# One decoder layer on one NeuronCore: constant pool shortened by 128 bytes, RWKV output splits and first down products in another order

## The chip, the core and the metric

The kernel runs on one NeuronCore of a Trainium2 chip. Its time is the device time of one launch in microseconds (us), read on the chip. The engines are named as the profile names them: PE (TensorE, matrix products), PEld (the loads of PE's stationary operand, which run beside products), DVE (VectorE), ACT (ScalarE), POOL (GpSimd) and SP (SyncE, here the issuer of nearly all DMA transfers). Each engine runs its own instruction list in order, and lists meet at semaphores.

## The reference, cut to what matters

```python
h = rms_norm(x, norm1_w) * (1 + sc1) + sh1          # x: (512, 1024), sc/sh/gt from c @ w_ada
proj = h @ w_in                                      # attention, RWKV and gate columns
y_att = attention_mixer(att_in) @ w_att_out
y_rwkv = rwkv7_mixer(rwkv_in, ...) @ w_rwkv_out
x = x + gt1 * ((sig(g_att) * y_att + sig(g_rwkv) * y_rwkv) @ w_o)
h = rms_norm(x, norm2_w) * (1 + sc2) + sh2
u = conv_b + sum(conv_w[j] * shifted(h @ w_up)[j])   # w_up: (1024, 5632), causal width 3
x = x + gt2 * ((silu(u_gate) * u_val) @ w_down)      # w_down: (2816, 1024)
out = rms_norm(x, norm_f_w)
```

All of it is float32. The kernel keeps that precision by splitting each operand of the large products into a rounded high part and the remainder, and by adding three products: high by high, high by low, low by high.

## The kernel before, in words

**Products.** A large product takes 128 rows of contraction at a time; the moving operand has 512 columns, the stationary one 128. `gemm_ks` (lines 432 to 439) and `tok_gemm` issue the three products per 128 rows, all through line 415, so the profile groups them by tile names: `u<-h2hi,whi` is a product into u with h2hi moving and whi stationary. In the up projection the activations h2 move and the weights stand; in the down projection and the `w_o` product the weights move and the activations (f, mhi and mlo) stand.

**Weight splits.** `load_w` brings 512 KB of raw weights into the ring `raw` (two buffers, pool `wp`). `split_w` (lines 456 to 462) has ACT copy the high part (line 460) and DVE subtract it for the low part (line 461). The results go into `whi` and `wlo`, two buffers each, which come free when PE has used them.

**Memory.** Pools stand at the left-hand end of SBUF, one behind the other, or at the right-hand end. The first left-hand pool, `cp`, holds constants; `vec_rest` (lines 531 to 555) makes nine scaled copies of parameter columns in it. All left-hand pools behind it (weights, `hp` with the first norm's output, `fp` with f) start where `cp` ends. The right-hand pools hold h2, the RWKV output y (`yhi`, `ylo`), and the extra weight buffers `we` of the last down products.

**RWKV output.** `rwkv_out` runs with an order written out by hand. For the eight 128-column blocks m of the mixed output, PE multiplies y by `w_rwkv_out` (`pr`), DVE applies the gate (`added`, line 2441), adds the attention branch (line 2445), ACT makes mhi (line 2446), and DVE makes mlo (line 2449). Between them stand the splits of the `w_rwkv_out` blocks 5 to 7, of the eight row blocks of `w_o` (`split_wo`), and of the first `w_up` blocks. `mix_out` then forms the four token blocks n of `(...) @ w_o`, the residual, the second norm and, through transposes on PE (line 418), h2: DVE scales into `hf` (line 626), ACT copies h2hi (line 631), POOL subtracts h2lo (line 632). The residual tile x of n = 0 lies where the gate tiles of m = 6 and 7 were, so its load on SP (line 2532) waits for the last use of these, the mlo of m = 7.

**FFN.** `ffn_first` does the first up block for 384 tokens, then the last 128 tokens when their h2 is there. `ffn_up` runs over f = 0 to 21; for each f two halves z (gate and value), each 24 products, then the convolution on ACT and DVE (`u`, lines 2599 and 2601), SiLU, and the split of f into fhi and flo. In the iteration f = 20 stands the split of the first `w_down` row block, from a raw buffer of its own (`rawd`) in the pool `up`; a scheduler places each instruction in its engine's list, and this one stands early, as the lists below show. `ffn_down` accumulates over 22 row blocks k for four token blocks n, two halves each, in eight PSUM banks, two of which hold the last `u` until DVE has read it. The first eight (k, n) pairs stand in a written order.

Of the kernel before, what the change touches and what calls it, by code (L numbers as in the profile page):

```python
# [19 lines left out]
P = 128  # L20
S = 512
D = 1024
# [373 lines left out]
class Layer:  # L396
# [134 lines left out]
    def vec_rest(self, deps):  # L531
# [3 lines left out]

        def scaled(name, m, a):
            s = self.col[name]
            o = cp.tile([P, s.shape[1]], F32, name=self.n(name))
            todo.append((o, s, m, a))
            return o  # L540

        self.omu = scaled("mu", -1.0, 1.0)
        self.omu2 = scaled("mu2", -1.0, 1.0)
        self.w0h = scaled("w0", 0.5, 0.0)
        self.a0h = scaled("a0", 0.5, 0.0)
        self.kkn = scaled("k_k", -1.0, 0.0)
        self.kkh = scaled("k_k", 0.5, 0.0)
        self.kah = scaled("k_a", 0.5, 0.0)
        self.kao = scaled("k_a", -0.5, 1.0)
        self.bgh = scaled("b_gate", 0.5, 0.0)  # L550

# [1871 lines left out]
    def rwkv_out(self, mpool, wpool, psp):  # L2423
# [15 lines left out]
        def added(m):  # L2439
            t, pr = self.tr_[m], ahead[m]["pm"]  # L2440
            nc.vector.scalar_tensor_tensor(t, t, 1.0, pr, op0=ALU.add, op1=ALU.mult)

        def mixed(m):
            t = self.tr_[m]
            nc.vector.tensor_tensor(t, t, self.p[m], op=ALU.add)
            nc.scalar.activation(self.mhi[:, m, :], t, AF.Copy, scale=0.5)
# [5 lines left out]
        with self.tc.manual_schedule(engines={T.PE, T.DVE, T.Activation, T.Pool, T.SP}):  # L2452
# [27 lines left out]
            for m in range(3, KD):  # L2480
                if m > 4:
                    ahead[m]["pm"] = psp("pr")
                prod(ahead[m]["w"], ahead[m]["pm"], range(KD))
                if m == 5:
                    ahead.append(dict(w=self.split_w(raw)))
                self.split_wo()
                if m + 1 < KD:
                    self.load_wo(wpool, m + 1)
                if m == KD - 1:
                    self.split_wo()  # L2490
                added(m)
                mixed(m)
                mixed_lo(m)
# [96 lines left out]
    def ffn_up(self, fp, up, psx):  # L2590
# [13 lines left out]
        for f in range(NFF):  # L2604
# [5 lines left out]
            if f == NFF - 2:  # L2610
                raw = self.load_w(self.w_down[0][:P, :], 1, D, up, tag="rawd", bufs=1)
                self.fp, self.wd0 = fp, [x[:, 0, :] for x in self.split_w(raw, pool=fp, tag="wd")]
            us = [conv(z, f, pus[z]) for z in range(2)]
# [4 lines left out]
    def ffn_down(self, xp, op, psx):  # L2618
# [9 lines left out]
        w = {0: self.wd0, 1: self.row_w(self.w_down[0], 1)}  # L2628
        for k, n in ((0, 0), (0, 1), (0, 2), (1, 0), (0, 3), (1, 1), (1, 2), (1, 3)):
            self.tok_gemm(pt[n], n, fk, w, [k], NFF)  # L2630
# [182 lines left out]
```

## Time and profile before

| what | value |
|---|---|
| median of three runs | 1175.56 us (1174.59 to 1177.84) |
| the profiled execution's own time | 1174.78 us |
| its span, first to last instruction | 1173.1 us |
| PE busy | 1156.1 us, 99% |
| DVE, ACT, POOL busy | 739.2, 536.1, 134.9 us |
| up projection, f = 1 to 21 | 810.12 to 1044.36 us of the span |
| down projection | 1044.36 us to the end |
| mean granted TensorE clock | 0.997 |

How to read it: a row of the timeline has start, duration, engine, source line, operation and tiles, and in brackets the idle time before it with what ended it. Durations of products are modelled and overlap the next one; the time that a product costs in a dense run is the distance between starts. A span on PE that is 99% busy can hence still hold products that start later after each other than others do.

### The profile page before, as it was taken

The numbers are of one execution on the slowest core, as the hardware profiler recorded it, in microseconds if no ns is written. First come the engines' busy times: TensorE is split into PE (matmuls) and PEld (weight loads), VectorE is DVE, ScalarE is ACT, GpSimd is POOL, SyncE is SP. The second block draws the span as 40 slices with busy tenths as digits, with TensorE's granted clock in tenths as the row PEclk, the third lists the DMA queues.
The fourth block names the chain that finished last, engine by engine and source line by source line (L and its number), as shares of the span: only waits on it lengthen the run. The fifth ranks groups of instructions, "written<-read, shape, count | busy, mean of one in ns | idle before, by whom it ended". The sixth has DMA issues, their size and how long they took to land.

```text
span 1173.1 us, 18932 instructions
## 1 busy us (share of the span) xinstructions
PE 1156.1 (99%) x7432; PEld 927.9 (79%) x7432; DVE 739.2 (63%) x1268; ACT 536.1 (46%) x1013; POOL 134.9 (12%) x272
## 2 busy tenths in 40 slices
PE   9999999999999999999999999999999999999997
PEld 7888887887777777778777668788888888878886
DVE  6788756315799968458996456755656556542236
ACT  5566526216564554455365553445444444432123
POOL 6000000001200033221003330032000000000001
PEclk9999999999999999999999999999999999999999
DMA  9656663311342423223223536611333333332331
GB/s 363 216 179 222 218 212 109 92 37 44 99 113 64 117 86 108 67 84 103 74 74 115 157 114 228 203 55 54 91 90 94 104 90 90 97 101 90 94 122 73
DMA packets 161820, 139.01 MB, mean 118 GB/s; under 512 B 8513, under 2 KB 141761, under 8 KB 161730
## 3 DMA queue, kind: packets, MB, share of 16 engines
q1 hardware_dynamic: 161586, 137.47, 37.7%
q8 instruction: 58, 0.95, 0.3%
q14 instruction: 32, 0.26, 0.1%
q10 hardware_dynamic: 144, 0.33, 0.1%
HBM read 127.47 MB, written 10.30 MB: 117 GB/s over the span
## 4 chain that ended last, share of the span: by engine, by line
PE 46%; DVE 3%; issue 1%; ACT 1%; DMA 0%; POOL 0%; POOLq 0%; DVEq 0%; ACTq 0%
PE u L415 21%; PE o L415 12%; PE pr L415 3%; PE pg L415 3%; PE pa L415 2%; PE xy L415 1%; PE xo L415 1%; PE pe L415 1%; DMA raw<-in_w_o_dram 0%; DVE tt L1839 0%; DVE tt L1837 0%; PE t L415 0%; DVE wlo L461 0%; DVE hf L626 0%; DVE wlo L1462 0%
## 5 line engine op out<-in xcount | busy, mean ns | idle before, releaser
L461 DVE TENSOR_TENSOR wlo<-raw,whi 128x1024 fp32r<-128x1024 f32 x64 | 78.4, 1224 | 145.6 <-ACT whi L460 145.6
L415 PE MATMUL u<-h2hi,whi 128*128 128x512 f32 (+2 forms) x364 | 141.7, 389 | 0.8 <-ACT h2hi L631 0.8
L415 PE MATMUL u<-h2lo,whi 128*128 128x512 f32 (+2 forms) x364 | 141.7, 389 | 0.2 <-POOL h2lo L632 0.2
L415 PE MATMUL u<-h2hi,wlo 128*128 128x512 f32 (+2 forms) x364 | 141.5, 389 | 0.0
L1462 DVE TENSOR_TENSOR wlo<-raw,whi 128x1024 fp32r<-128x1024 f32 (+1 forms) x73 | 84.5, 1158 | 45.7 <-ACT whi L1459 45.2
L460 ACT CAST whi<-raw 128x1024 fp32r<-128x1024 f32 x64 | 67.1, 1049 | 99.2 <-PE o L415 54.8
L1459 ACT CAST whi<-raw 128x1024 fp32r<-128x1024 f32 (+1 forms) x73 | 72.4, 993 | 69.8 <-PE qk L415 11.2
L415 PEld LDWEIGHTS u<-h2hi,whi 128*128 128x128 f32 x364 | 68.6, 188 | 15.9 <-ACT h2hi L631 1.1
L415 PEld LDWEIGHTS u<-h2lo,whi 128*128 128x128 f32 x364 | 68.6, 188 | 15.3 <-POOL h2lo L632 0.3
L415 PEld LDWEIGHTS u<-h2hi,wlo 128*128 128x128 f32 x364 | 68.6, 188 | 15.0
L571 DVE CUSTOM_DVE_ANT_0 araw<-araw,cb,cols 128x1024 f32<-128x1024 f32 x48 | 61.4, 1287 | 15.4 <-DMA araw<-in_w_ada_dram 15.3
L2601 DVE SCALAR_TENSOR_TENSOR u<-u,cols,u 128x511 f32<-128x511 f32 x88 | 65.6, 746 | 1.5
L415 PE MATMUL qk<-hhi,whi 128*128 128x512 f32 x160 | 64.1, 406 | 0.2
L415 PE MATMUL qk<-hhi,wlo 128*128 128x512 f32 x160 | 62.8, 395 | 0.0
L415 PE MATMUL qk<-hlo,whi 128*128 128x512 f32 x160 | 62.6, 396 | 0.0
L415 PE MATMUL o<-whi,fhi 128*128 128x512 f32 x136 | 52.9, 389 | 0.0
L415 PE MATMUL o<-wlo,fhi 128*128 128x512 f32 x136 | 52.9, 389 | 0.0
L415 PE MATMUL o<-whi,flo 128*128 128x512 f32 x136 | 52.9, 389 | 0.0
L415 PE MATMUL pg<-hhi,whi 128*128 128x512 f32 x128 | 51.7, 411 | 1.0 <-DVE k L1472 0.8
L415 PE MATMUL pg<-hlo,whi 128*128 128x512 f32 x128 | 51.5, 408 | 0.0
L415 PE MATMUL pg<-hhi,wlo 128*128 128x512 f32 x128 | 50.7, 405 | 0.0
L1112 ACT ACTIVATE pr<-sm,stat 128x256 f32<-128x256 f32 (+1 forms) x64 | 31.4, 491 | 36.2 <-PE pt L418 19.8
(465 smaller groups left out, 2729.1 us busy)
## 6 DMA issues: line engine op xcount, KB each, us to landing
raw<-in_w_in_dram SPq DMA_DIRECT2D x62, 512.0 KB, 3.9
araw<-in_w_ada_dram SPq DMA_DIRECT2D x48, 512.0 KB, 5.8
raw<-in_w_up_dram SPq DMA_DIRECT2D x44, 512.0 KB, 3.6
raw<-in_w_down_dram SPq DMA_DIRECT2D x22, 512.0 KB, 3.4
wvraw<-in_w_in_dram SPq DMA_DIRECT2D x20, 256.0 KB, 4.1
raw<-in_w_rwkv_out_dram SPq DMA_DIRECT2D x8, 512.0 KB, 4.5
raw<-in_w_o_dram SPq DMA_DIRECT2D x8, 512.0 KB, 4.1
gate_d<-gs SPq DMA_DIRECT2D x15, 256.0 KB, 2.1
```

The source lines that it names most:

```text
L415: return self.nc.tensor.matmul(out, lhsT, rhs, start=start, stop=stop)
L460: self.nc.scalar.copy(hl[0], raw)
L461: (lo_eng or self.nc.vector).tensor_tensor(hl[1], raw, hl[0], op=ALU.subtract)
L571: self.nc.vector.tensor_tensor_reduce(raw, raw, self.cb, 1.0, self.col["b_ada"][:, m : m + 1], op0=ALU.mult, op1=ALU.add, accum_out=col)
L1112: nc.scalar.activation(d["pr"][h][:, :wd], d["sm", h][:, :wd], AF.Exp, bias=stt[gi][:, n, 0, hd(h) : hd(h) + 1], scale=-1.0, accum_out=stt ...
L1459: nc.scalar.copy(d["w"][0], d["raw"])
L1462: nc.vector.tensor_tensor(d["w"][1], d["raw"], d["w"][0], op=ALU.subtract)
L2601: nc.vector.scalar_tensor_tensor(u[:, d:], pu[:, : S - d], ch(c), u[:, d:], op0=ALU.mult, op1=ALU.add)
```

## The change

Three edits.

1. Three of the nine scaled columns (w0, a0, b_gate) are written in place over their source columns instead of into new tiles. `cp` becomes 32 + 32 + 64 = 128 bytes per partition shorter, and every left-hand pool behind it moves down by 128 bytes. Right-hand pools stay. In the built programs the tiles of the large products then start as follows (address modulo 256 bytes, moving / stationary):

| product | before | after |
|---|---|---|
| up, f = 1 to 21 (h2 / w) | 128 / 0 | 128 / 128 |
| up, f = 0, z = 0 (h2 / w) | 128 / 0 | 128 / 128 |
| up, f = 0, z = 1 (h2 / w of a right-hand pool) | 128 / 128 | 128 / 128 |
| down, k = 0 to 18 (w / f) | 0 / 0 | 128 / 128 |
| down, k = 19 to 21 (we / f) | 128 / 0 | 128 / 128 |
| RWKV output (y / w) | 128 / 0, for most | 128 / 128, for most |
| `w_o` product (wo / m) | 0 / 0 | 128 / 128 |
| projections by `w_in` (h / w) | 0 / 0 | 128 / 128 |

Counting, over the whole program, the 512-column moving operand of one product against the stationary operand of the next product: 2241 pairs agree modulo 256 before and 3561 after; 1471 are 128 apart before and 151 after. Of the 1471, 1009 are in the up projection, 165 in the RWKV output, 79 in the attention output (`pa`), 63 in the down projection.

2. In `rwkv_out` the products of m = 5 are written ahead with those of m = 4, and with them the split of the last `w_rwkv_out` block (m = 7); the last `w_o` split is written behind the gate steps of m = 7. PE's order of the `pr` products is the same as before. DVE's list around the gate steps of m = 4, first before, then after (`wlo<-raw,whi` in the first rows is the split for m = 7, wolo those of `w_o`, gate and mlo the gate steps):

```order
L2449 SCALAR_TENSOR_TENSOR mlo<-gate_7576,mhi 128x512
L2309 TENSOR_TENSOR wolo_7720<-raw_7659,wohi_7719 128x1024
L2441 SCALAR_TENSOR_TENSOR gate_7577<-gate_7577,pr_7598 128x512
L2445 TENSOR_TENSOR gate_7577<-gate_7577,gate_6991 128x512
L2449 SCALAR_TENSOR_TENSOR mlo<-gate_7577,mhi 128x512
L461 TENSOR_TENSOR wlo_7755<-raw_7657,whi_7754 128x1024
```

```order
L2449 SCALAR_TENSOR_TENSOR mlo<-gate_7573,mhi 128x512
L461 TENSOR_TENSOR wlo_7742<-raw_7654,whi_7741 128x1024
L2309 TENSOR_TENSOR wolo_7746<-raw_7656,wohi_7745 128x1024
L2441 SCALAR_TENSOR_TENSOR gate_7574<-gate_7574,pr_7595 128x512
L2445 TENSOR_TENSOR gate_7574<-gate_7574,gate_6988 128x512
L2449 SCALAR_TENSOR_TENSOR mlo<-gate_7574,mhi 128x512
```

The split for m = 7 moved ahead of four instructions. At the end of this stage the two first `w_up` splits move ahead of the gate steps of m = 6, the last wolo stands between the add and the mlo of m = 7, and mlo of m = 7 is still the last of them. In PE's list, three products of n = 1 move between those of n = 0 and the ones that need the last `w_o` block.

3. The first `w_down` block uses the shared `raw` ring instead of a buffer of its own, and the first down products run in another (k, n) order. DVE's list ahead of the last token block's `hf`, before and after (wdlo is the low part of the first `w_down` block):

```order
L2551 TENSOR_TENSOR x_3_8154<-x_3_8154,xo_8158 128x512
L563 TENSOR_TENSOR vv_8257<-ss_8160 128x1
L565 TENSOR_SCALAR vv_8257<-vv_8257 128x1
L461 TENSOR_TENSOR wdlo_9906<-raw_9903,wdhi_9905 128x1024
L626 TENSOR_SCALAR hf_8322<-tr_8317,g1c,sh_115 128x128
```

```order
L2552 TENSOR_TENSOR x_3_8151<-x_3_8151,xo_8155 128x512
L563 TENSOR_TENSOR vv_8254<-ss_8157 128x1
L565 TENSOR_SCALAR vv_8254<-vv_8254 128x1
L626 TENSOR_SCALAR hf_8319<-tr_8314,g1c,sh_115 128x128
L626 TENSOR_SCALAR hf_8323<-tr_8314,g1c,sh_115 128x128
```

The split leaves this place on DVE; on ACT the copy wdhi leaves the same place, and on SP the load leaves its place ahead of the third up block's. They now stand in the iteration f = 20. There DVE's list after is:

```order
L461 TENSOR_TENSOR wlo_9873<-raw_9870,whi_9872 128x1024
L2602 SCALAR_TENSOR_TENSOR u_9830<-u_9765,cols,u_9830 128x511
L461 TENSOR_TENSOR wdlo_9903<-raw_9900,wdhi_9902 128x1024
L2602 SCALAR_TENSOR_TENSOR u_9830<-u_9765,cols,u_9830 128x510
L2615 TENSOR_TENSOR u_9826<-u_9826,u_9830 128x512
L2309 TENSOR_TENSOR flo<-u_9826,fhi 128x512
L2602 SCALAR_TENSOR_TENSOR u_9906<-u_9838,cols,u_9906 128x511
L2602 SCALAR_TENSOR_TENSOR u_9906<-u_9838,cols,u_9906 128x510
L461 TENSOR_TENSOR wlo_9923<-raw_9920,whi_9922 128x1024
```

The last row, the low part for f = 21, z = 0, stood ahead of the two `u` rows above it before. The first down products on PE, rows 13 to 24 of that stage before and after (wdhi and wdlo are block k = 0, whi and wlo block k = 1; o_10014 and o_10015 are the halves of n = 2, o_10010 and o_10011 those of n = 0; after, o_10007 and o_10008 are n = 0, o_10011 and o_10012 n = 2):

```order
L415 MATMUL o_10014<-wdhi_9905,fhi 128x512
L415 MATMUL o_10014<-wdlo_9906,fhi 128x512
L415 MATMUL o_10014<-wdhi_9905,flo 128x512
L415 MATMUL o_10015<-wdhi_9905,fhi 128x512
L415 MATMUL o_10015<-wdlo_9906,fhi 128x512
L415 MATMUL o_10015<-wdhi_9905,flo 128x512
L415 MATMUL o_10010<-whi_10020,fhi 128x512
```

```order
L415 MATMUL o_10007<-whi_10017,fhi 128x512
L415 MATMUL o_10007<-wlo_10018,fhi 128x512
L415 MATMUL o_10007<-whi_10017,flo 128x512
L415 MATMUL o_10008<-whi_10017,fhi 128x512
L415 MATMUL o_10008<-wlo_10018,fhi 128x512
L415 MATMUL o_10008<-whi_10017,flo 128x512
L415 MATMUL o_10011<-wdhi_9902,fhi 128x512
```

Six products of k = 1 now stand ahead of those of n = 2.

```diff
-        def scaled(name, m, a):
+        def scaled(name, m, a, keep=True):
             s = self.col[name]
-            o = cp.tile([P, s.shape[1]], F32, name=self.n(name))
+            o = cp.tile([P, s.shape[1]], F32, name=self.n(name)) if keep else s
...
-        self.w0h = scaled("w0", 0.5, 0.0)
-        self.a0h = scaled("a0", 0.5, 0.0)
+        self.w0h = scaled("w0", 0.5, 0.0, False)
+        self.a0h = scaled("a0", 0.5, 0.0, False)
...
-        self.bgh = scaled("b_gate", 0.5, 0.0)
+        self.bgh = scaled("b_gate", 0.5, 0.0, False)
...
             for m in range(3, KD):
-                if m > 4:
-                    ahead[m]["pm"] = psp("pr")
-                prod(ahead[m]["w"], ahead[m]["pm"], range(KD))
-                if m == 5:
-                    ahead.append(dict(w=self.split_w(raw)))
+                for p in ((3,), (4, 5), (), (6,), (7,))[m - 3]:
+                    if p > 4:
+                        ahead[p]["pm"] = psp("pr")
+                    prod(ahead[p]["w"], ahead[p]["pm"], range(KD))
+                    if p == 5:
+                        ahead.append(dict(w=self.split_w(raw)))
                 self.split_wo()
                 if m + 1 < KD:
                     self.load_wo(wpool, m + 1)
+                added(m)
+                mixed(m)
                 if m == KD - 1:
                     self.split_wo()
-                added(m)
-                mixed(m)
                 mixed_lo(m)
...
             if f == NFF - 2:
-                raw = self.load_w(self.w_down[0][:P, :], 1, D, up, tag="rawd", bufs=1)
-                self.fp, self.wd0 = fp, [x[:, 0, :] for x in self.split_w(raw, pool=fp, tag="wd")]
+                self.fp, self.wd0 = fp, self.row_w(self.w_down[0], 0, pool=fp, tag="wd")
...
-        for k, n in ((0, 0), (0, 1), (0, 2), (1, 0), (0, 3), (1, 1), (1, 2), (1, 3)):
+        for k, n in ((0, 0), (0, 1), (1, 0), (0, 2), (1, 1), (0, 3), (1, 2), (1, 3)):
```

## The prediction

> **What bounds the kernel now.** I read the page first: busy times, then the chain that ended last, then PE's groups with shapes kept apart, then PE's timeline where groups of the same shape differ.
>
> ```profile
> PE 1156.1 (99%) x7432; PEld 927.9 (79%) x7432; DVE 739.2 (63%) x1268; ACT 536.1 (46%) x1013; POOL 134.9 (12%) x272
> PE u L415 21%; PE o L415 12%; PE pr L415 3%; PE pg L415 3%; PE pa L415 2%; PE xy L415 1%; PE xo L415 1%; PE pe L415 1%; DMA raw<-in_w_o_dram 0%; DVE tt L1839 0%; DVE tt L1837 0%; PE t L415 0%; DVE wlo L461 0%; DVE hf L626 0%; DVE wlo L1462 0%
> ```
>
> PE is busy for 99% and the chain that ended last runs over its products u and o. So an edit gains only if PE's products start closer together, or if one of PE's few waits goes. The groups (count, busy us, mean ns, idle before) show the first:
>
> ```profile
> L415 PE MATMUL u<-h2hi,whi 128*128 128x512 f32 x340 | 134.2, 395 | 0.0
> L415 PE MATMUL o<-whi,fhi 128*128 128x512 f32 x136 | 52.9, 389 | 0.0
> L415 PE MATMUL o<-wehi,fhi 128*128 128x512 f32 x21 | 8.3, 394 | 0.0
> ```
>
> Three groups of one shape, none with idle time, but 395, 389 and 394 ns. The down projection has both kinds: with weights from the left-hand pools 389, with weights `we` from the right 394. By the table of addresses the 389 are equal modulo 256 bytes, the 394 and 395 are 128 apart. Starts tell it better than modelled durations. PE's timeline at the change from the second half of f = 0 (128 / 128) to f = 1 (128 / 0), and the end of the up projection:
>
> ```profile
> 807.61 0.39 PE L415 MATMUL u<-h2lo,whi 128*128 128x512 f32 x1
> ...
> 809.66 0.39 PE L415 MATMUL u<-h2lo,whi 128*128 128x512 f32 x1
> 809.88 0.40 PE L415 MATMUL u<-h2hi,wlo 128*128 128x512 f32 x1
> 810.12 0.40 PE L415 MATMUL u<-h2hi,whi 128*128 128x512 f32 x1
> 810.36 0.40 PE L415 MATMUL u<-h2lo,whi 128*128 128x512 f32 x1
> ...
> 1044.36 0.39 PE L415 MATMUL o<-wdhi,fhi 128*128 128x512 f32 x1
> ```
>
> From 807.61 to 809.88 lie ten steps of 227.0 ns, in the same stage, with the same moving tile as the rest. From 810.12, the first product of f = 1, to 1044.36 lie 21 x 2 x 24 = 1008 steps of (1044.36 - 810.12) / 1008 = 232.4 ns. The step grows at 809.88 already, whose own operands agree but under which the stationary operand of f = 1 is loaded: so it is the running product against the next load that matters, and that is how I count pairs.
>
> **The change part by part.** *Addresses, up projection.* 1008 products go from 232.4 to 227.0 ns: 1008 x 5.4 = **5.4 us**. The bounds: nothing, if the twelve fast products have another cause, and 6 us if the slow ones lose a little more than the mean of the fast ones shows. I take 5.4, since the two kinds of row meet at 809.88 with nothing else changed. The other engines must keep up; DVE is 63% busy, and the rows of f = 20 further down show its idle time there.
>
> [...]
>
> *Addresses, down projection.* 63 `we` products at 394 - 389 = 5 ns: **0.3 us**. The 2241 pairs that agreed before agree after, at 128 instead of 0. RWKV output and attention output products, 165 and 79 of them, could give 244 x 5.4 = 1.3 us; they lie in stages with waits, so I count them with edit 2.
>
> *The moved first down split.* DVE, ACT and PE at the second norm of the last token block, and PE and DVE at the block before it for comparison:
>
> ```profile
> 790.84 1.04 PE L418 MATMUL tr<-ident,xn 128*128 128x128 f32 x8
> 799.73 1.03 PE L418 MATMUL tr<-ident,xn 128*128 128x128 f32 x8
> 801.31 0.33 PE L415 MATMUL u<-h2lo,whi 128*128 128x384 f32 x1
> 801.48 0.34 PE L415 MATMUL u<-h2hi,wlo 128*128 128x384 f32 x1
> 802.59 0.33 PE L415 MATMUL u<-h2hi,whi 128*128 128x128 f32 x1 [0.77 <-ACT h2hi L631]
> 803.13 0.33 PE L415 MATMUL u<-h2lo,whi 128*128 128x128 f32 x1 [0.21 <-POOL h2lo L632]
> 803.29 0.28 PE L415 MATMUL u<-h2hi,wlo 128*128 128x128 f32 x1
> ```
> ```profile
> 791.55 1.37 DVE L626 TENSOR_SCALAR hf<-tr,g1c,sh 128x128 f32<-128x128 f32 x4 [1.82 <-PE tr L418]
> 800.66 1.22 DVE L461 TENSOR_TENSOR wdlo<-raw,wdhi 128x1024 fp32r<-128x1024 f32 x1 [3.04 <-ACT wdhi L460]
> 801.80 2.96 DVE L626 TENSOR_SCALAR hf<-tr,g1c,sh 128x128 f32<-128x128 f32 x8
> 802.24 2.85 ACT L631 CAST h2hi<-hf 128x128 fp32r<-128x128 f32 x8 [1.61 <-DVE hf L626]
> ```
>
> At the block before, hf starts 0.71 us after the transposes; here 2.07 us after, because wdlo stands ahead of it. Without wdlo hf starts 1.36 us earlier, so h2hi starts at 800.88 and its product could start at 801.23; PE gets there at 801.66, and no longer waits. PE loses 802.59 - 801.48 = 1.11 where 0.17 is normal, then 0.54 where 0.16 is: 0.94 + 0.38 = **1.3 us**, all of which goes. Less is possible if POOL's h2lo becomes the next to be late: its first product could start at 803.13 - 1.36 = 801.77, PE needs it at about 801.8, so at worst 0.3 us stays. The split's new place, f = 20, costs DVE 1.22 us and ACT about as much. DVE there, before:
>
> ```profile
> 1023.10 1.22 DVE L461 TENSOR_TENSOR wlo<-raw,whi 128x1024 fp32r<-128x1024 f32 x1 [2.92 <-ACT whi L460]
> 1028.68 1.23 DVE L461 TENSOR_TENSOR wlo<-raw,whi 128x1024 fp32r<-128x1024 f32 x1 [0.80 <-ACT whi L460]
> ```
>
> DVE idles 2.92 + 0.80 us around it, so 1.22 fits. The second row is the split for f = 21, z = 0, which now queues behind two u rows and ends perhaps 2 us later, at about 1032. PE needs it one block after its buffer came free (1027.6 by the idle row), that is 24 x 0.227 = 5.45 us later, at 1033.0. I count nothing; if that cover fails, 1 us.
>
> *The order of the first down products.* PE, then DVE:
>
> ```profile
> 1047.53 0.39 PE L415 MATMUL o<-wdhi,flo 128*128 128x512 f32 x1
> 1048.22 0.47 PE L415 MATMUL o<-wdhi,fhi 128*128 128x512 f32 x1 [0.30 <-DVE u L2601]
> 1048.53 0.40 PE L415 MATMUL o<-wdlo,fhi 128*128 128x512 f32 x1
> ```
> ```profile
> 1039.83 1.23 DVE L461 TENSOR_TENSOR wlo<-raw,whi 128x1024 fp32r<-128x1024 f32 x1 [0.81 <-ACT whi L460]
> 1046.55 1.53 DVE L2601 SCALAR_TENSOR_TENSOR u<-u,cols,u 128x511 f32<-128x511 f32 x2
> ```
>
> The second half of n = 2 waits for a PSUM bank that DVE reads until 1048.08. The steps 0.69 and 0.31 instead of 0.227 lose 0.46 + 0.08 = **0.5 us**. With six products of k = 1 ahead, n = 2 starts at 1044.36 + 18 x 0.227 = 1048.45, after the bank is free; the split of k = 1 (1039.83) is done by 1041.1. All of it goes.
>
> *RWKV output.* PE, then the chain behind it:
>
> ```profile
> 741.19 0.40 PE L415 MATMUL pr<-ylo,whi 128*128 128x512 f32 x1
> 742.11 0.50 PE L415 MATMUL pr<-yhi,wlo 128*128 128x512 f32 x1 [0.52 <-DVE wlo L461]
> 757.35 0.50 PE L415 MATMUL o<-wohi,mhi 128*128 128x512 f32 x1 [0.32 <-ACT mhi L2446]
> 767.28 1.04 PE L418 MATMUL tr<-ident,xn 128*128 128x128 f32 x8
> ```
> ```profile
> 757.33 0.69 DVE L2449 SCALAR_TENSOR_TENSOR mlo<-gate,mhi 128x512 fp32r<-128x512 f32 x1 [0.70 <-ACT mhi L2446]
> 758.05 1.76 SPq L2532 DMA_DIRECT2D x<-in_x_dram  x4
> 763.05 1.29 DVE L2551 TENSOR_TENSOR x<-x,xo 128x512 f32<-128x512 f32 x2 [3.05 <-DMA x<-in_x_dram]
> 766.24 1.34 ACT L2557 ACTIVATE xn<-x,rs 128x512 f32<-128x512 f32 x2 [1.13 <-POOL rs L567]
> ```
>
> The wlo of m = 7 moves ahead of four DVE instructions, so the wait at 742.11 (0.92 where 0.23 is normal) goes; with the shorter waits at 757.35 up to 1.7 us of PE's time can close here. But PE reaches the transposes at 767.28 without a wait, and the xn that they read ends its second half at 767.58: there is hardly any slack. That xn hangs on the load of x at 758.05, which waits for mlo of m = 7 (ended 758.02). That stays the last of DVE's gate list; filling the list in its new order with the durations of these rows, it ends some 0.4 us later, since the last wolo now stands between. So what PE gains ahead of the transposes it waits for at the transposes. Bounds for edit 2 with the pr and pa products: +1.7 + 1.3 = 3 us gained if x's load lands early enough, 0.8 us lost if mlo comes later and the load takes as long. I take **0.2 us** gained, near the end at which the transposes decide.
>
> **Sum.** 5.4 + 0.3 + 1.3 + 0.5 + 0.2 = 7.7 us, from the profiled execution's own 1174.78 us: **1167.0 us**. That execution was 0.8 us under the median of the runs; the same offset would put the median after at 1167.9.
>
> One thing is in no term. A window of the trace has a lower granted clock (columns: length, PE, PEld, DVE, ACT, POOL, PEclk, DMA):
>
> ```profile
> 645.00:655.00 10.00, 8.99 (x190) 6.89 (x190) 4.71 (x10) 5.49 (x14) 2.46 (x5) 0.83 0.71 224
> ```
>
> 0.17 x 10 = 1.7 us of clock are lost once, in the RWKV tail. A shifted program can lose it again or not at all; it widens the range by 1.7 us on both sides.
>
> **Rivals.** *Addresses don't matter*, and the twelve fast products have another cause, or the pools do not do what the edit says: then 1.3 + 0.5 + 0.2 remain, 1172.8 us. [...] For it: the 232.4 ns come with a stage in which DMA and splits run; against it: `we` in the down projection and the twelve products in the up projection differ from their own neighbours. 5%.
>
> *A wait takes the place*: x's load comes late and PE stands at the transposes (0.8 us lost), and the f = 20 split makes PE wait (1 us): 1167.0 + 0.2 + 0.8 + 1.0 = 1169.0 us. For it: no slack at 767.28. 10%.
>
> *128 is itself the slow residue*, on the other side: if a product pays for a stationary operand at 128 rather than for the difference, the 2241 pairs that go from 0 / 0 to 128 / 128 pay 5.4 ns each, 12.1 us, u gains nothing, and with the 2.0 us of the orders it is 1184.9 us. It decides once more than 7.7 / 0.0054 = 1430 pairs pay. For it: only twelve rows of the trace are 128 / 128. Against it: these twelve are as fast as the 0 / 0 rows, 227.0 ns. 3%.
>
> **How the numbers follow.** The forecast holds 82%, with a range of its own of 1164 to 1169.5 us; the rivals 5, 10 and 3%. The range 1163.5 to 1171.5 takes in the second rival, the clock loss and edit 2's gain; it leaves out the first and third rival and part of each tail. A measurement tells apart 0.3%, 3.5 us: the forecast and the second rival lie beyond it (92%), the first within (5%), the third is slower (3%).
>
> **What would show it.** The u groups at 389 ns and 227 ns from start to start over f = 1 to 21, `we` at 389; any u stage still at 232 ns makes the prediction wrong by 5.4 us. No wdlo ahead of hf, and no PE wait for h2hi. No wait for DVE u in the first down products. In the RWKV output no wait for wlo, but one ahead of the transposes of n = 0. PE waits near f = 21 would show the moved split uncovered, and 232 ns in the w_in or w_o products would show the third rival.

## The result, and the profile after

| | before | after |
|---|---|---|
| median, us | 1175.07 (1172.32 to 1177.84, 4 runs) | 1164.49 (1163.93 to 1167.37, 4 runs) |
| profiled execution, its own time and span, us | 1174.78, 1173.1 | 1163.93, 1162.2 |
| PE busy, us | 1156.1 | 1146.3 |

The ratio is 0.9915, with an interval of 0.9886 to 0.9944: 10.6 us faster by the medians, where 1167.0 us had been forecast for the profiled execution. Beside the later kernels, before and after were timed again: 63 runs of the kernel before have a median of 1174.42 us, and six more runs of the changed kernel one of 1164.18 us.

Each run comes with its mean granted PE clock: 37 of those 63 runs of the kernel before show 0.996 or less, with a median of 1175.72 us, the other 26 show more, with 1172.50 us, and no run of the changed kernel shows less than 0.997. The experiments on the wait deal with that.

The page after, busy times, and the same groups of products as before (count, busy us, mean ns, idle before):

```profile
PE 1146.3 (99%) x7432; PEld 925.8 (80%) x7432; DVE 739.0 (64%) x1268; ACT 536.3 (46%) x1013; POOL 135.2 (12%) x272
```
```profile
L415 PE MATMUL u<-h2hi,whi 128*128 128x512 f32 x340 | 132.4, 389 | 0.0
L415 PE MATMUL o<-whi,fhi 128*128 128x512 f32 x136 | 52.9, 389 | 0.0
L415 PE MATMUL o<-wehi,fhi 128*128 128x512 f32 x21 | 8.2, 389 | 0.0
```

All three kinds stand at 389 ns now. PE is as busy as it was, 99%; only its instructions follow each other more closely. Where the time went is told best by the starts of the same products in the two traces. Before, those that the prediction does not show:

```profile
697.62 0.50 PE L415 MATMUL pr<-yhi,whi 128*128 128x512 f32 x1
...
1055.79 0.39 PE L415 MATMUL o<-whi,fhi 128*128 128x512 f32 x1
```

After, the first `pr` product, the transposes of n = 2, the first product of f = 1, the first down product, and the one 48 products later:

```profile
695.33 0.50 PE L415 MATMUL pr<-yhi,whi 128*128 128x512 f32 x1
...
788.02 0.27 PE L418 MATMUL tr<-ident,xn 128*128 128x128 f32 x1
...
805.94 0.39 PE L415 MATMUL u<-h2hi,whi 128*128 128x512 f32 x1
...
1034.42 0.39 PE L415 MATMUL o<-wdhi,fhi 128*128 128x512 f32 x1
...
1045.30 0.39 PE L415 MATMUL o<-whi,fhi 128*128 128x512 f32 x1
```

| stretch | before, us | after, us | gained, us | forecast, us |
|---|---|---|---|---|
| start to the first `pr` product | 697.62 | 695.33 | 2.29 | in no term |
| to the transposes of n = 2 (RWKV output, `w_o`) | 93.22 | 92.69 | 0.53 | 0.2 |
| to the first product of f = 1 (last split) | 19.28 | 17.92 | 1.36 | 1.3 |
| up projection, f = 1 to 21 | 234.24 | 228.48 | 5.76 | 5.4 |
| first 48 down products | 11.43 | 10.88 | 0.55 | 0.5 |
| the other down products (`we` among them) | 109.18 | 108.83 | 0.35 | 0.3 |
| sum | | | 10.84 | 7.7 |

The five terms together are 8.55 us where 7.7 had been forecast. Of the 2.29 us ahead of them 2.1 arise between 644 and 659 us of the span. These are the clock of 645 to 655 us, where the trace after has 1.00 for 0.83:

```profile
645.00:655.00 10.00, 9.59 (x207) 7.18 (x204) 4.56 (x10) 6.55 (x17) 4.24 (x8) 1.00 0.80 239
```

and a pause of 1.01 us on PE ahead of it, of which the trace before says only "issue", and which the trace after does not have:

```profile
648.45 0.22 PE L415 MATMUL pe<-lr,gt 32*32 32x32 f32 x2 [1.01 <-issue]
```

In the list of PE's waits after, those for h2hi, h2lo and `u` are gone, and in the RWKV output those for wlo and mhi. Two of 0.7 us each stand in the RWKV output instead (us in total, times, longest):

```profile
PE o L415 <- ACT wohi L2309: 0.7, 1, 0.7
PE tr L418 <- ACT xn L2558: 0.7, 1, 0.7
```

At the moved split, hf starts without wdlo ahead of it, and PE goes from the products of 384 tokens to those of the last 128 without a stop (802.59 - 801.48 = 1.11 us before, 798.79 - 798.62 = 0.17 now):

```profile
798.62 0.34 PE L415 MATMUL u<-h2hi,wlo 128*128 128x384 f32 x1
798.79 0.22 PE L415 MATMUL u<-h2hi,whi 128*128 128x128 f32 x1
798.92 0.33 PE L415 MATMUL u<-h2lo,whi 128*128 128x128 f32 x1
```

### The profile page after: what moved, and what is told of

Its sections match the earlier page's. It is cut to its first block, busy times and chain, and to the rows that moved or that the text cites. A ratio compares the mean times of both kernels' runs of the same rounds, so it can differ in the third digit from the quotient of the medians.

```text
span 1162.2 us, 18932 instructions
## 1 busy us (share of the span) xinstructions
PE 1146.3 (99%) x7432; PEld 925.8 (80%) x7432; DVE 739.0 (64%) x1268; ACT 536.3 (46%) x1013; POOL 135.2 (12%) x272
```

## Experiments: the addresses

**One part each.** The addresses alone, that is edit 1 in the kernel before; and the orders alone, that is the changed kernel with 128 bytes put back:

```diff
+        cp.tile([P, 32], F32, name=self.n("pad"))
```

> The kernel before with edit 1 alone (three scaled columns in place, left-hand pools 128 bytes lower), orders as before. Theory: what counts is the running product's moving operand against the next stationary operand, modulo 256 bytes. Then the up products step at 227 ns and the stage f = 1 to 21 is 5.4 to 5.8 us shorter than before, the we products give 0.3 us, and the waits of the orders stay (PE for wlo in the RWKV output, for h2hi ahead of f = 0, for u in the first down products): about 6.3 us faster than the kernel before, some 1168.8 us. Rival, addresses don't matter and the twelve fast products have another cause: the up products stay at 232 ns and the time at that of before.

> The changed kernel with 128 unused bytes put back into the constant pool, so that left-hand pools lie where they lay before: edits 2 and 3 alone. Theory: the up products step at 232 ns as before, the wait for h2hi (1.3 us) and the one in the first down products (0.5 us) are gone, the wait for wlo in the RWKV output is gone too but one ahead of the transposes of n = 0 stands in its place, 0 to 0.5 us net: 1.8 to 2.3 us faster than before, some 1173 us. Rival, the gain came from the orders and not from the addresses: 227 ns steps and some 8 us faster. A clock window of 0.17 x 10 us at 645 to 655 us may stand here or not; if it stands here and not with the addresses changed, it belongs to the addresses.

The addresses alone: 1166.99 us, ratio 0.9949 (0.9932 to 0.9966). The orders alone: 1169.58 us, ratio 0.9957 (0.9945 to 0.9970); the kernel before, beside them, 1174.65 us. The group of the orders alone is what it was before the change, 395 ns, and so is `we`:

```profile
L415 PE MATMUL u<-h2hi,whi 128*128 128x512 f32 x340 | 134.2, 395 | 0.0
L415 PE MATMUL o<-wehi,fhi 128*128 128x512 f32 x21 | 8.3, 394 | 0.0
```

With the addresses alone, the up projection runs from

```profile
813.39 0.39 PE L415 MATMUL u<-h2hi,whi 128*128 128x512 f32 x1
...
1041.88 0.39 PE L415 MATMUL o<-wdhi,fhi 128*128 128x512 f32 x1
```

which is 228.49 us, as in the changed kernel (228.48); with the orders alone it takes 234.24, as before. So this stage hangs on the addresses alone. At a clock of 0.997 or more the medians are 1172.50 before, 1166.54 with the addresses, 1169.58 with the orders and 1164.18 with both: 6.0 and 2.9 us, and 8.3 together. The orders alone gain more than the 1.8 to 2.3 us expected. The stretches of their trace, taken as in the table above, give only 1.33 + 0.55 - 0.04 = 1.84 us, but that execution took 1170.42 us, 0.84 over the median of its runs.

**Every offset.** Is it 128 that costs, or any difference? Here the high part of each weight block is written into a tile 256 bytes longer, at an offset that changes with f and with k; h2, wlo and f stay as in the changed kernel, so that one product in three keeps its agreement. To make room, an output buffer near the end of the program has three copies in place of four. In the second kernel h2 is moved by 128 bytes as well.

```diff
+        hi = fp.tile([P, 1024 + 64], F32R, tag="wu", bufs=2, ...)[:, off // 4 : off // 4 + 1024]
```

> The changed kernel with the high weights of f = 2 to 21 and of down blocks k = 2 to 17 in a ring of their own, each f and each k at another byte offset: up 0, 4, 8, 16, 24, 32, 48, 64, 80, 96, 112, 128, 144, 160, 176, 192, 208, 224, 240, 0; down 0, 8, 16, 32, 64, 96, 128, 160, 192, 224, 240, 0, 128, 64, 192, 0. Low weights stay at offset 0. Theory: within one block the step behind the product of whi and h2lo, whose next stationary operand is wlo at offset 0, stays at 227 ns in every f, while the other two steps grow with the offset, to 232 ns at 128; whether the cost is a threshold within 256 bytes or a ramp is open, and 0 at the end returns to 227. In the down blocks the same with the moving operand shifted. Rival, absolute address or the stage: all three steps of a block move together, or none.

> The same sweep with both h2 tiles moved by 128 bytes, so that the moving operand of the up products is at 0 and the weights at 128 plus the offset. Theory (difference modulo 256): the whole pattern moves by 128. The step with wlo as the next stationary operand is slow, 232 ns, in every f, the other two are slow at offset 0 and fast, 227 ns, at offset 128. Rival (the absolute residue of the stationary operand decides, 128 being the fast one): the pattern of the sweep before, fast at offset 0. The down blocks repeat the sweep before.

1169.3 and 1171.17 us, one run each. The starts of f = 2 (offset 0), f = 3 (offset 4), f = 4, f = 21 (offset 0 again) and of the first down product in the first of the two:

```profile
816.24 0.39 PE L419 MATMUL u<-h2hi,wu 128*128 128x512 f32 x1
...
827.12 0.39 PE L419 MATMUL u<-h2hi,wu 128*128 128x512 f32 x1
...
838.22 0.39 PE L419 MATMUL u<-h2hi,wu 128*128 128x512 f32 x1
...
1027.21 0.40 PE L419 MATMUL u<-h2hi,wu 128*128 128x512 f32 x1
...
1038.12 0.39 PE L419 MATMUL o<-wdhi,fhi 128*128 128x512 f32 x1
```

48 products take 10.88 us at offset 0 (226.7 ns each) and 11.10 at offset 4. All twenty, from the same view:

| offset, bytes | 0 | 4 | 8 | 16 | 24 | 32 | 48 | 64 | 80 | 96 |
|---|---|---|---|---|---|---|---|---|---|---|
| 48 products, us | 10.88 | 11.10 | 11.09 | 11.20 | 11.06 | 11.13 | 11.14 | 11.09 | 11.19 | 11.05 |

| offset, bytes | 112 | 128 | 144 | 160 | 176 | 192 | 208 | 224 | 240 | 0 |
|---|---|---|---|---|---|---|---|---|---|---|
| 48 products, us | 11.09 | 11.20 | 11.16 | 11.11 | 11.04 | 10.99 | 11.10 | 11.19 | 11.16 | 10.91 |

Only agreement is free. One element of difference costs 0.22 us per 48 products, two thirds of the 0.32 us at 128 bytes; there is no order by size, and 128 is one of the dearest but nothing special. The expectation that the step with wlo as the next stationary operand would stay at 227 ns missed: at offset 128 the three steps of a group have means of 233.2, 232.2 and 234.5 ns, so that all three move, which had been named as the sign of the rival (the absolute address, or the stage). The second kernel, below, tells the two apart. The down projection has the moving operand shifted instead. The starts of k = 13 (offset 0), 14 (offset 128) and 15:

```profile
1110.14 0.39 PE L419 MATMUL o<-wu,fhi 128*128 128x512 f32 x1
...
1115.58 0.40 PE L419 MATMUL o<-wu,fhi 128*128 128x512 f32 x1
...
1121.08 0.39 PE L419 MATMUL o<-wu,fhi 128*128 128x512 f32 x1
```

24 products: 5.44 us at offset 0, 5.50 at 128; the other offsets have 5.54 to 5.63. The second kernel repeats these stages to 0.02 us, so that the cost is no scatter. It is not the same on both sides: 128 bytes cost 0.06 us of 24 products here and 0.32 of 48 where the weights stand. (One stage at offset 0, k = 17, took 5.48 us in both kernels; why is open.)

With h2 moved, all three products of a group are 128 apart in f = 1, and two of three agree in f = 13, whose offset is 128:

```profile
805.98 0.40 PE L419 MATMUL u<-h2hi,whi 128*128 128x512 f32 x1
...
817.18 0.40 PE L419 MATMUL u<-h2hi,wu 128*128 128x512 f32 x1
...
939.81 0.39 PE L419 MATMUL u<-h2hi,wu 128*128 128x512 f32 x1
940.04 0.40 PE L419 MATMUL u<-h2lo,wu 128*128 128x512 f32 x1
...
950.91 0.40 PE L419 MATMUL u<-h2hi,wu 128*128 128x512 f32 x1
```

11.20 us for the one, 11.10 for the other. So offset 0 has become slow (11.20 in f = 1, 11.21 in f = 2), and the rival, by which the address of the weights alone decides, falls. The kernel before has the same difference of 128 bytes in all three products, with h2 at 128 and the weights at 0, and takes 234.24 / 21 = 11.15 us; why 0.05 less is open. In f = 13 only the first step of each group is at its low value (940.04 - 939.81 = 0.23 us; over the stage the three have a mean of 226.7, 232.4 and 234.5 ns). The third step's own pair agrees, and it is the slowest, which the expectation (227 ns) did not have. The reading that fits both sweeps is that one pair that does not agree delays the step behind it too: a count of pairs gives the right sum where all agree or none do, and too small a loss where one in three does not.

So in the first sweep the same products take 226.7 to 227.3 ns each at offset 0 (10.88 and 10.91 us for 48) and 229.0 to 233.3 ns at the others (10.99 to 11.20 us), by the offset alone.

## Experiments: the orders

**The RWKV order taken back**, the other edits kept:

```diff
-                for p in ((3,), (4, 5), (), (6,), (7,))[m - 3]:
-                    if p > 4:
-                        ahead[p]["pm"] = psp("pr")
...
+                if m > 4:
+                    ahead[m]["pm"] = psp("pr")
...
-                added(m)
-                mixed(m)
                 if m == KD - 1:
                     self.split_wo()
+                added(m)
+                mixed(m)
```

> The changed kernel with the RWKV output's order as before; addresses and FFN edits stay. Nothing is left out. Theory of the prediction: that order is worth 0.2 us, since the transposes of n = 0 wait for x either way: about 1164.7 us, 0.2 over the changed kernel (1164.5). Theory from the traces of the two halves: without the order the shorter pr and o products run into the wait for wlo of m = 7 and the third and fourth wait again (with the addresses alone the stage from the last pe product to the transposes of n = 1 took 125.81 us, with both edits 125.03): about 0.8 us over the changed kernel, 1165.3 us. Either way PE should wait for wlo of m = 7 in the pr products again.

1165.06 us (1164.56 to 1166.20), 0.9 over the 1164.18 of the changed kernel and 0.6 over its first median, 1164.49: nearer to the 1165.3 of the theory from the traces than to the 1164.7 of the prediction's. PE's waits of the kernel before are back, with one for whi that the kernel before did not have:

```profile
PE pr L415 <- ACT whi L460: 0.8, 1, 0.8
PE pr L415 <- DVE wlo L461: 0.5, 1, 0.5
PE o L415 <- ACT mhi L2446: 0.4, 1, 0.4
```

The stretch from the first `pr` product to the transposes of n = 2 says what the order is worth. With the old order it takes 93.22 us (before), 93.36 (addresses alone) and 93.63 (this kernel); with the new order and the new addresses 92.69 to 93.13 in eight traces, 92.9 in the mean; with the new order and the old addresses 93.26. So the order gains some 0.6 us with the agreeing addresses. With the addresses alone the waits for whi, wlo and mhi add up to 0.7 + 0.5 + 0.6 = 1.8 us, where the kernel before has 0.5 + 0.3, and that eats what the faster products gain in this stretch. Whether the order gains nothing with the old addresses, as 93.26 beside 93.22 would have it, is not shown: it is one trace each, eight traces of one order and addresses lie 0.44 us apart, and the medians of the parts (6.0 and 2.9) add up to more than the whole (8.3), not to less.

**The end of that stage.** Where do those scattered tenths come from? The load of x for n = 0, DVE's add that takes it, and the transposes, in the changed kernel:

```profile
756.17 1.76 SPq L2533 DMA_DIRECT2D x<-in_x_dram  x4
```
```profile
759.76 1.30 DVE L2552 TENSOR_TENSOR x<-x,xo 128x512 f32<-128x512 f32 x2 [1.70 <-DMA x<-in_x_dram]
```
```profile
764.22 1.27 PE L418 MATMUL tr<-ident,xn 128*128 128x128 f32 x8 [0.68 <-ACT xn L2558]
```

From the load's issue to the add it takes 3.6 us here and 5.0 before (763.05 - 758.05). Two kernels take away what the load waits for: the residual tile of n = 0 is put where gate tiles that are used up earlier were; in the second the last `w_o` split also goes back ahead of the gate steps of m = 7.

```diff
+        slots = [xp.tile([P, D], F32, name=f"x1_{n}", tag=f"x1_{n}") for n in (3, 0, 1, 2)]
+        slots = slots[1:] + slots[:1]
...
-            x1 = xp.tile([P, D], F32, name=f"x1_{n}", tag=f"x1_{n}")
+            x1 = slots[n]
```

> The changed kernel with the residual tile of token block 0 where the gate tiles of m = 3 and 5 were, and that of block 3 in its old place, so that the load of x for n = 0 need not wait for mlo of m = 7. Nothing is left out. Theory (the transposes of n = 0 wait for x, which waits for mlo of m = 7): PE's 0.7 us wait for xn ahead of them goes, 1163.8 us, 0.7 under the changed kernel. Rival (xn waits for the o products of n = 0 and the norm's chain anyway): no difference, 1164.5 us.

> As the one with the residual tiles moved, and the last split of w_o ahead of the gate steps of m = 7, as it was before the change. Nothing is left out. Theory: PE's wait for the high part of the last w_o block (0.7 us, before o of n = 0) goes too, and 1.3 us in all: 1163.1 us. Rival: DVE's gate steps of m = 7 come 1.2 us later for it, mhi of m = 7 is late instead, and PE waits there: 1163.8 us or more.

The first: 1164.23 us (1162.90 to 1164.96), no gain that these runs can tell. Its load is issued 7 us earlier, and the add no longer waits for it; but PE still waits 0.33 us at the transposes, for xn:

```profile
749.26 6.46 SPq L2535 DMA_DIRECT2D x<-in_x_dram  x4
```
```profile
763.15 1.27 PE L418 MATMUL tr<-ident,xn 128*128 128x128 f32 x8 [0.33 <-ACT xn L2560]
```

It is not x that xn waits for now, but DVE's order. ACT has the sums of squares of n = 0 ready at 759.28; the step of the norm that takes them (vv) stands in DVE's list behind the first product of the next token block (xo), which waits for PE:

```profile
760.13 0.69 DVE L2553 TENSOR_TENSOR xo<-o,gt1b 128x512 f32<-128x512 f32 x1 [1.63 <-PE o L415]
760.74 0.15 DVE L563 TENSOR_TENSOR vv<-ss 128x1 f32<-128x1 f32 x1
```

In the second kernel vv stands ahead of that product and starts at 759.47.

The second: 1163.50 us (1162.27 to 1165.08), ratio to the kernel before 0.9905 (0.9887 to 0.9923), beside 0.9910 (0.9884 to 0.9937) for the changed kernel. Its wait at the transposes is gone and its stretch is the shortest, 91.74 us; the wait for the high part of the last `w_o` block has turned into one for mhi, as the rival had it:

```profile
PE o L415 <- ACT mhi L2446: 1.0, 1, 1.0
```

It stands between the theory's 1163.1 and the rival's 1163.8. The intervals of the two kernels lie over each other, so that a version better than the changed kernel is not shown.

## Experiments: the wait ahead of the last 128 tokens

**The down split taken back**, with its own raw buffer, everything else as changed:

```diff
-                self.fp, self.wd0 = fp, self.row_w(self.w_down[0], 0, pool=fp, tag="wd")
+                raw = self.load_w(self.w_down[0][:P, :], 1, D, up, tag="rawd", bufs=1)
+                self.fp, self.wd0 = fp, [x[:, 0, :] for x in self.split_w(raw, pool=fp, tag="wd")]
```

> The changed kernel with the first down split back at its early place (its own raw buffer, wdlo ahead of the last hf on DVE). Nothing is left out. Theory of the prediction: 1.3 us over the changed kernel, 1165.8 us, with PE's waits for h2hi and h2lo at the first up block of the last 128 tokens back. Rival: the wait is only moved, and PE waits near f = 21 in the changed kernel instead: no difference, 1164.5 us. On the clock: if a half-clock window comes after a PE pause of about 1 us (before: 1.0 us pause and then 3.4 us at half clock; with the addresses alone 1.1 us for h2hi and then 6.8 us at half clock), some runs stand 3.4 us over the others, as this wait is back; if windows come with the late instruction fetch near 645 us only, this kernel has no more of them than the changed one.

1167.09 us, but in two groups: three runs at 1164.4 to 1165.4 us with a clock of 0.998, three at 1168.8 to 1170.0 us with 0.995 or 0.996. The profiled execution is one of the first. In it wdlo stands ahead of hf again, and PE waits again:

```profile
797.41 1.23 DVE L461 TENSOR_TENSOR wdlo<-raw,wdhi 128x1024 fp32r<-128x1024 f32 x1 [3.03 <-ACT wdhi L460]
```
```profile
799.34 0.33 PE L415 MATMUL u<-h2hi,whi 128*128 128x128 f32 x1 [0.80 <-ACT h2hi L631]
```

From the transposes of n = 2 to f = 1 it takes 19.31 us, 1.39 more than the changed kernel: the term of 1.3. The other group is what the sum had no term for. The addresses alone had this wait too, and three of their ten runs stood at 1171.3 to 1172.2 us with 0.993 to 0.996; its profiled execution was one of them, and shows twice what the trace before shows once, a stretch in which the granted clock is 0.50 (length, PE, PEld, DVE, ACT, POOL, PEclk; before, then the addresses alone):

```profile
649.50:652.91 3.41, 3.41 (x48) 2.44 (x49) 1.70 (x5) 2.63 (x7) 0.00 (x0) 0.50 0.64 201
```
```profile
648.98:652.39 3.41, 3.41 (x26) 2.23 (x27) 1.39 (x2) 2.62 (x8) 0.00 (x0) 0.50 0.58 190
801.99:805.99 4.00, 3.14 (x24) 2.98 (x25) 2.81 (x8) 2.39 (x8) 3.32 (x8) 1.00 0.00 0
805.99:812.82 6.83, 6.83 (x24) 5.96 (x24) 2.63 (x3) 1.72 (x2) 0.05 (x1) 0.50 0.06 16
812.82:816.82 4.00, 4.00 (x19) 3.28 (x19) 1.97 (x3) 2.70 (x3) 0.00 (x0) 1.00 0.35 104
```

Half clock for 6.83 us costs 3.4 us by its length; the stretch from the transposes of n = 2 to f = 1 takes 22.48 us here, 3.2 more than with the split taken back. It begins at 805.99, 3.3 us after PE's wait for h2hi ended at 802.65:

```profile
802.65 0.33 PE L415 MATMUL u<-h2hi,whi 128*128 128x128 f32 x1 [0.81 <-ACT h2hi L631]
```

**The wait without the split.** Is it the wait, or the early split and its transfer? The changed kernel with one, two or four idle DVE products ahead of hf, whose result is not used (of the four, two ended up behind the first and the second hf in DVE's list):

```diff
+            if spare is not None and kq == 0 and n == NT - 1:
+                for _ in range(2):
+                    nc.vector.tensor_tensor(spare, xn, spare, op=ALU.mult)
```

> The changed kernel with one idle DVE product of 128x1024 (its result is not used) ahead of the first hf of the last token block, where the first down split stood before. Nothing is left out. Theory (the half-clock windows near 806 us come after PE's wait of 1.1 us for h2hi, whatever causes it): a median of 1.3 us over the changed kernel at full clock, 1165.8 us, and in a good part of the runs 3.4 to 5 us more with a mean granted clock of 0.996 or less. Rival (the windows come with the early split or its transfer themselves): 1165.8 us, and no run with a clock under 0.997.

> As the one before, with two such DVE products, so that PE waits about 2.4 us at the same place. Nothing is left out. Theory of the wait: 1.3 + 1.2 = 2.5 us over the changed kernel at full clock, 1167.0 us, and windows in as many runs as with one product or in more. Rival: 1167.0 us in all runs, clock 0.998.

> The changed kernel itself beside the two with the pause, on the same chip. By both theories 1164.5 us and no run with a clock under 0.997; if it shows such runs too, neither the wait nor the split sets them.

> As the one with two idle DVE products, with four, so that PE's wait at that place is some 2.4 us longer, about 3.8 us. Nothing is left out. At full clock 1166.0 + 2.4 = 1168.4 us. Theory of the wait: runs with a mean granted clock of 0.996 or less in half of the runs or more, and, if the profiled execution is one of them, its half-clock window starts within 5 us behind the wait, near 807 us of the span. Rival (such runs are chance on the chip and no matter of the wait): none or few, as in the kernels without the wait, where none of the timed runs had a clock under 0.997.

| kernel | transposes of n = 2 to f = 1, us | runs with a clock of 0.996 or less | median of those, us | median of the others, us |
|---|---|---|---|---|
| changed kernel, again | 17.93 | 0 of 6 | | 1164.18 |
| one idle product | 18.38 | 1 of 6 | 1169.47 | 1164.59 |
| down split taken back | 19.31 | 3 of 6 | 1169.60 | 1164.94 |
| two idle products | 19.63 | 6 of 11 | 1169.39 | 1166.03 |
| four idle products | 24.89 (with half clock) | 12 of 12 | 1171.35 | |

One idle product makes hardly any wait (PE waits 0.20 us, for h2lo), less than expected, since it starts sooner than wdlo did. Two make a wait somewhat longer than that of the kernel before (1.13 us for 0.77), though not the 2.4 us expected, and six of eleven runs have the lower clock, with no split near:

```profile
800.46 0.33 PE L415 MATMUL u<-h2hi,whi 128*128 128x128 f32 x1 [1.13 <-ACT h2hi L634]
```

With four PE waits 1.15 us for h2hi and twice more for h2lo, and the clock drops in every run. Its trace shows where:

```profile
801.02 0.33 PE L415 MATMUL u<-h2hi,whi 128*128 128x128 f32 x1 [1.15 <-ACT h2hi L634]
802.13 0.33 PE L415 MATMUL u<-h2lo,whi 128*128 128x128 f32 x1 [0.79 <-POOL h2lo L635]
```
```profile
800.52:804.52 4.00, 2.38 (x15) 1.92 (x16) 4.00 (x9) 1.49 (x5) 2.63 (x4) 1.00 0.00 0
804.52:814.76 10.24, 10.24 (x38) 9.08 (x37) 3.38 (x5) 2.61 (x5) 1.97 (x5) 0.50 0.17 48
814.76:818.76 4.00, 4.00 (x19) 3.33 (x18) 2.19 (x3) 3.04 (x4) 0.00 (x0) 1.00 0.02 7
```

10.24 us at half clock, from 804.52 on, with PE never idle in them: half of it, 5.1 us, is lost behind 2.3 us of waiting (1.15 + 0.79, and 0.33 later). The expected 1168.4 us at full clock was never measured, since no run had it.

Over all kernels: those without the wait (the changed one, the orders alone, both sweeps, the RWKV order taken back, both with moved x tiles) have none of 40 runs at 0.996 or less; those with it (before, the addresses alone, the split taken back, two and four idle products) 61 of 102. The 61 hold runs that lost the clock near 650 us, as the profiled one of the kernel before did, which kept full clock behind this wait. The last three kernels differ from the changed one only by what makes the wait, and have 21 of 29. So the wait sets it off, whether the split or idle products make PE wait; that the clock falls right behind it is seen in two traces, those of the addresses alone and of the four products, since the profiled executions of the other two kept full clock. (One idle product, with its short wait, lies between: 1 of 6.)

The three lengths at half clock, 3.41, 6.83 and 10.24 us, stand as one to two to three: 6.83 / 3.41 = 2.00 and 10.24 / 3.41 = 3.00. Ahead of the drop stands a wait of 0.81 us for h2hi with the addresses alone, and waits of 1.15, 0.79 and 0.33 us with the four products. In the same kernel some runs show the lower clock and others do not (three of six with the split taken back, six of eleven with two idle products); what decides it is not shown, and no run here tries it.

Two more things stay open. The waits of 0.7 us in the RWKV output never set it off, and why this place does and those do not was not tried; products of 128 columns with waits between them keep PE busy for 2.38 of 4.00 us ahead of the drop above. That share alone does not decide it: with the split taken back PE is busy for 2.41 of the 3.42 us from 796.45 to 799.87, and with the RWKV order taken back for 2.04 of the 3.41 us from 737.58 to 740.99, and both keep full clock behind it. And the window near 650 us, in the traces of the kernel before and of the addresses alone, follows a pause that the trace puts down to "issue". In those two a 16 KB fetch of instructions that began near 644.5 us took 2.6 and 2.2 us, by the records of single packets, and the pause is 1.01 and 0.72 us. A third trace fits: with h2 moved the fetch took 1.75 us, and PE pauses 0.18 us at the same products, with no drop behind it; in the other eleven it took 0.9 to 1.7 us, with no such pause. So the pause grows with this fetch (the next one, near 649 us, took 2.4 us in the second kernel with moved x tiles and brought none), but that the fetch is PE's and that PE stood for it is only argued, and nothing in the change touches that place.

## Why the prediction was right, and where it was off

**The bound** was right: what was gained are PE's products closer together and waits of PE that went.

**Addresses, up projection**, 5.4 forecast, 5.76 measured. That the steps hang on the addresses held in both halves of the change (228.49 us with the addresses alone, 234.24 with the orders alone) and in the sweep (10.88 us for 48 products at offset 0, 10.99 to 11.20 at the eighteen others). The size was a little low because the slow mean was set against 227.0 ns, read from ten steps; the 1008 steps after have 228.48 / 1008 = 226.7 ns. The upper bound of 6 us held. What the count of pairs has wrong, and the forecast didn't need, is that a pair that does not agree seems to cost the next step too (234.5 ns, with h2 moved and offset 128, for the step whose own pair agrees).

**`we`**, 0.3 forecast, 0.35 measured (63 products from 394 to 389 ns; from the first `we` product to the last, narrower ones among them, 21.46 to 21.11 us).

**The moved first down split**, 1.3 forecast, 1.36 measured, 1.39 when taken back alone. POOL's h2lo did not become the next to be late, and its new place in f = 20 made PE wait nowhere. The step that failed stands behind the sum: of the clock the prediction says "A shifted program can lose it again or not at all", and gives it no term. The lower clock is not chance alone: the runs with idle products show that this wait sets it off, and 37 of the 63 runs of the kernel before have it. (How many of the 37 had it at this place and how many near 650 us, as the profiled one, their traces would have to tell.) So the medians of the longer series lie 1174.42 - 1164.18 = 10.2 us apart, and 8.3 at the same clock: 1174.42 - 1172.50 = 1.9 us of the median before were the lower clock, of which nothing is left.

**The order of the first down products**, 0.5 forecast, 0.55 measured. PE no longer waits for `u` there.

**RWKV output**, 0.2 forecast, 0.53 measured in the trace, 0.6 over all traces and 0.6 to 0.9 by the runs. That PE would stand at the transposes instead was right (0.68 us, for xn). The value was taken near the bound at which the load of x takes as long as before, 5.0 us; it took 3.6. Issued 0.4 us later relative to its stage, as forecast, it still came back earlier; the other kernels with the new order and this load have 3.5 to 3.9 us (759.33 - 755.65 with the down split taken back, 760.09 - 756.32 with the orders alone), those with the old order 4.0 to 5.4. Why it comes back sooner in the new order is not shown. PE's wait of 0.7 us for the high part of the last `w_o` block stood in no term.

**The rivals.** That addresses don't matter fell with the addresses alone, at 228.49 us for the up projection; its time, 1172.8 us, lies 8.3 us over the median. That a wait takes the place was half right: the wait at the transposes came, 0.7 us, with another of 0.7 us that it did not name, but inside the gain; the one near f = 21 did not come. That 128 itself is slow fell too: with everything at 128 the steps are 226.7 ns, and with the high weights moved away from it they are slower (229.0 to 233.3 ns).

**The time.** 1167.0 us was 3.1 us over the profiled execution after: 0.85 us are the five terms, and 2.29 us nearly all the half clock and the pause ahead of it, which the profiled execution before had and the one after has not. The median, 1164.49, and the profiled 1163.93 lie at the lower end of the range. At the same clock the gain is 8.3 us, close to the 7.7 forecast; that the clock would add to it was not forecast.

## What to carry to other kernels

Where 512-column products follow each other, compare the address of the moving operand with that of the next stationary one modulo 256 bytes, and lay out pools so that they agree: here each difference tried, from 4 to 240 bytes, cost 1 to 4% of the products (10.99 to 11.20 us for 10.88 in the up projection, 5.50 to 5.63 for 5.44 in the down projection). A wait of one microsecond on PE between thin products can cost several more of half clock behind it, in only a part of the runs (here, with 1.13 us in the profiled execution of the kernel with two idle products, six of eleven runs have the lower clock, at a median of 1169.39 us for 1166.03); so look at the granted clock of each run, not only of the profiled one, before a loss is called chance. A product that waits for a late operand can give back what faster products ahead of it gain: with the addresses alone the stretch of the RWKV output and the `w_o` product was no shorter than before (93.36 us for 93.22, one trace each).

## What the runs showed of the hardware that was not expected

- The cost of disagreeing addresses has no order by size: 48 products took 10.88 us at offset 0, 11.10 at 4 bytes, 10.99 at 192 and 11.20 at 16 and 128, and in the down projection, where two kernels have the same offsets, it repeats to 0.02 us.
- While PE has work, the granted clock falls to half for 3.41, 6.83 or 10.24 us, up to 3.5 us behind a PE wait or pause of 0.7 to 1.15 us, though PE is busy the whole time that it is low. The more waiting, the surer: none of 40 runs without the wait, 1 of 6 with one idle product, 6 of 11 with two, 12 of 12 with four.
- The two kernels whose clock fell near 650 us had a 16 KB fetch of instructions that took 2.2 and 2.6 us, and a PE pause of 0.7 and 1.0 us, in the middle of products of 32 columns; a third had 1.75 us, a pause of 0.18 us and no drop.
